# Mixed quarters of the feed-forward activations: t1 and t4 summed on TensorE like t2, ahead of the products of keys 3 and 4

## The chip, the core and the metric

The kernel runs on one core of a Trainium2 chip. The metric is device time of one execution in microseconds (us); lower is better. The engines are TensorE (PE, with PEld for its weight loads), VectorE (DVE), ScalarE (ACT), GpSimd (POOL) and SyncE (SP, which here only issues DMAs).

## What is computed

One decoder layer on a sequence of 1024 tokens with width 1024: attention and a state-space branch side by side, merged by gates and an output projection, and then a feed-forward block. The change lies in the feed-forward block. Of the reference it is these lines:

```
hn = rmsnorm(h, norm_ffn[i])
gate, up = jnp.split(hn @ w_ffn_in[i], 2, axis=-1)
h = h + (jax.nn.silu(gate) * up) @ w_ffn_out[i]
```

with `D_FF` = 2816, all in float32.

## The kernel before

Every product of the kernel is made of float32 operands that are split into a high part, rounded to the format fp32r, and a low part, the rest (`split`, L187: a cast on ACT, then a subtraction on DVE). `product` (L798) makes three matmuls for each block of 128 contracted rows: high with high, high with low, low with high.

The feed-forward products use a scheme of seven products instead of eight for a 2 x 2 block product. The normalized activations, transposed, lie in SBUF as quarters: `b11` and `b21` are the two halves of the features for tokens 0 to 511, `b22` is the second half of the features for tokens 512 to 1023, and `t3` is `b22` less the first half for those tokens; `norm_h` (L1106) makes these four, one block of 128 tokens at a time. From them come three mixed quarters: `t2 = b11 + t3`, `t1 = b22 - t2`, `t4 = b21 - t2`. Each is a tile of high and low parts, 128 partitions x 4 x 512 columns, in the dictionary `X`. The weights of a unit, 256 columns of `w_ffn_in`, are read in four quarters too (`raw_f`, later `raw_fg` for gate and `raw_fu` for up), and mixed on DVE into four sums (`sf`, `first_sums`). The seven products have the keys `11`, `12`, `2`, `3`, `1`, `22` and `4`; keys `11`, `12`, `3` and `4` need no mixed quarter of the activations but `t3`, key `2` needs `t2`, key `1` needs `t1`, key `22` needs `t4` (`FOR_B`, L796).

Units come in pairs, u = 0 for gate and u = 1 for up. The first pair (names ending in `_e`) is begun early, in the block that starts at L1098. Its keys `11` and `12` (banks `ch_e` and `si_e`, weights `we`) run between the last transposes of `norm_h`. Then stand, in the code's order: `t2`; for each u the loads, the sums, the operands (`wf`) and the products of keys `3` and `4` (banks `th_e` and `ex_e`); then operands and the quarters `t1` and `t4`. `first_units` (L1254) does the rest of the first pair: copies of the finished banks into cells (`c_e`, on ACT), then keys `2`, `1` (again in `ch_e`) and `22` (in `th_e`). From the second pair on `ffn_unit` (L1275) does a unit (names with `fg` and `fu`).

`mixed` (L833) makes a mixed quarter. For `t2` it sums on PE: for each of four groups of 512 columns it multiplies the high and low parts of both terms by an identity matrix, `one_r`, into one bank, four matmuls in all; ACT and DVE split the bank into the parts of `t2`, and ACT copies it once more, whole, into a page `t2f`. For `t1` and `t4` it works on DVE alone, on two halves of 1024 columns: high part of the other term less the page of `t2`, plus its low part, into a page (`t1f`, `t4f`), then a split.

The banks of PSUM, 128 partitions x 512 columns, are handed out in turn within four tags: `m` and `s` with two each, `x` with three and `q` with one. `th_e` of both units and `ex_e` of u = 0 are in `x`, `ex_e` of u = 1 is in `q`. Pages, the copies of the residual stream, the early weights and the raw weights of u = 1 share the pool `big` of eight tiles. A scheduler sets the order of the instructions on each engine from the code's order and the buffers; each engine then takes its own list strictly in that order.

Of the kernel before, what the change touches and what calls it, by code (L numbers as in the profile page):

```python
# [9 lines left out]
F32R = mybir.dt.float32r  # L10
I32 = mybir.dt.int32
BF16 = mybir.dt.bfloat16
AF = mybir.ActivationFunctionType
ALU = mybir.AluOpType
# [3 lines left out]
P = 128  # L18
# [28 lines left out]
def hybrid_layer_kernel(ctx: ExitStack, tc: tile.TileContext, x, meta_tokens, norm_mix, w_in, q_norm, k_norm,  # L47
                        attn_sinks, lam_re, lam_im, log_dt, ssm_b_re, ssm_b_im, ssm_c_re, ssm_c_im, ssm_d,
                        w_glu, attn_branch_norm, ssm_branch_norm, w_out, norm_ffn, w_ffn_in, w_ffn_out, out):
    nc = tc.nc  # L50
    x, out = x[0], out[0]
# [12 lines left out]
    def bank(name, tag=None):  # L64

        if tag is None:
            tag = "mmss"[turn[0] % 4]
            turn[0] += 1
        return ps.tile([P, 512], F32, tag=tag, bufs=BANKS[tag], name=name)
# [16 lines left out]
    ident = const.tile([P, P], F32, name="ident")  # L86
    make_identity(nc, ident)
    one_r = const.tile([P, P], F32R, name="one_r")
# [98 lines left out]
    def split(hi, lo, src):  # L187
        nc.scalar.copy(hi, src)  # L188
        nc.vector.tensor_tensor(out=lo, in0=src, in1=hi.bitcast(F32), op=ALU.subtract)
# [28 lines left out]
    with sbuf("p1", 2) as p1:  # L218
# [43 lines left out]
        pt = bank("lamT", "x")  # L262
# [26 lines left out]
        for b, (k, n) in enumerate([(ks[:, b, :], P) for b in range(8)] + [(ksm, NMETA)]):  # L289
            k = k.rearrange("p (h d) -> p h d", d=HD)  # L290
# [20 lines left out]
        t1, t2 = t12[:, 0:8], t12[:, 8:16]  # L311
# [91 lines left out]
    with sbuf("pp", 1) as pp:  # L403
# [26 lines left out]
        for what in range(2):  # L430
            raw = bc[what][:GRP].rearrange("g a b -> g (a b)")
            X, Y = ((XB, YB), (XC, YC))[what]
            for hh in range(2):
                pt = bank(f"bcT{what}{hh}", "x")
# [16 lines left out]
        for blk in range(8):  # L451
# [20 lines left out]
            for hh in range(2):  # L472
                pt = bank(f"bpT{blk}{hh}", "x")
# [14 lines left out]
            for e in range(2):  # L488
                for j in range(2):
                    o = bank(f"v{blk}{e}{j}", "q" if j else "x")  # L490
                    for k in range(2):
                        g = e + 4 * j + 2 * k
                        nc.tensor.matmul(o[:, k * NCH:(k + 1) * NCH], bpt[:, g * P:g * P + P], ut[:, g, :],
                                         start=True, stop=True)
# [277 lines left out]
    m = sp.tile([P, 2, 2, GRP // 2], F32, tag="cm", name="m")  # L772
# [33 lines left out]
    def tt_(out, in0, in1, op, eng=nc.vector):  # L806
        eng.tensor_tensor(out=out, in0=in0, in1=in1, op=op)  # L807

    X = {}
# [7 lines left out]
    def x_pair(key):  # L817

        t = rows_a(f"X{key}")
        X[key] = [t[:, 4 * p:4 * p + 4, :] for p in range(2)]  # L820
# [10 lines left out]

    full = {}

    def mixed(key, a, b, op, tag="s"):


        if key == "t2":
            for k in range(4):
                pt = bank(f"{key}_{k}", tag)
                for i, v in enumerate((X[b][0], X[b][1], X[a][0], X[a][1])):  # L840
                    nc.tensor.matmul(pt, one_r, v[:, k, :], start=(i == 0), stop=(i == 3))
                if k % 2 == 0:
                    full[k] = page(f"{key}f{k}").rearrange("p (k n) -> p k n", k=2)
                split(X[key][0][:, k, :], X[key][1][:, k, :], pt)
                nc.scalar.copy(full[k // 2 * 2][:, k % 2, :], pt)
            return
        for k in (0, 2):
            t = page(f"{key}f{k}").rearrange("p (k n) -> p k n", k=2)
            hi, lo = (X[a][p][:, k:k + 2, :].bitcast(F32) for p in range(2))
            tt_(t, hi, full[k], op)  # L850
            tt_(t, t, lo, ALU.add)
            split(X[key][0][:, k:k + 2, :], X[key][1][:, k:k + 2, :], t)
# [54 lines left out]
    for blk in (0, 4, 1, 5, 2, 6, 3, 7):  # L907
# [13 lines left out]
        for hh in range(2):  # L921
            o = bank(f"y{blk}{hh}")
            for k in range(4):
                g = 4 * hh + k
                nc.tensor.matmul(o[:, k * P:(k + 1) * P], ut[:, g, 2:], tp[:, :, g * 16:g * 16 + 16],
                                 start=True, stop=False)
                nc.tensor.matmul(o[:, k * P:(k + 1) * P], ss[:, g // 2, g % 2, :], ct[:, g, :],
                                 start=False, stop=True)
            nc.scalar.activation(
                out=z[:, :, 64 * hh:64 * hh + 64].rearrange("p t (g c) -> p g t c", c=16),  # L930
                in_=o.rearrange("p (g t c) -> p g t c", g=4, t=T), func=AF.Gelu_apprx_tanh)
# [13 lines left out]
    def page(name):  # L945
        return big.tile([P, D], F32, tag="s", name=name)

    with sbuf("mp", 2) as mp:
# [94 lines left out]
        for u in two:  # L1043
            for key in ("11", "12"):
                glu_step(*u, key, ops[u], True)
        mixed("t2", "t3", "b11", ALU.add)
        prepare(ua, "2", "3", "4")
        prepare(ub, "22", "2", "3", "4")
# [3 lines left out]
        for key, t, a in (("2", None, None), ("22", "t4", "b21"), ("1", "t1", "b22")):  # L1052
            if t:
                mixed(t, a, "t2", ALU.subtract)
            for u in two:
                if key == "1":
                    prepare(u, "1")
                glu_step(*u, key, ops[u], True)
# [41 lines left out]
    with sbuf("op", 2) as op_:  # L1100
        g_ffn = op_.tile([P, D], F32, tag="g", bufs=1, name="g_ffn")
        nc.scalar.dma_start(out=g_ffn, in_=norm_ffn[0:1, :].to_broadcast([P, D]))
        ssq = op_.tile([P, 8, 2], F32, tag="ssq", bufs=1, name="ssq")
        h2 = [None] * 8

        def norm_h(b):  # L1106
# [89 lines left out]
        def first_operands(u, keys, a, sums):  # L1196
            for key in keys:
                if key == "3":
                    src = op_.tile([P, 512], F32, tag="xs", bufs=3, name=f"sf3_{u}").rearrange("p (k n) -> p k n", k=4)
                    tt_(src, a["11"], a["21"], ALU.subtract)  # L1200
                elif key == "22":
                    src = a["22"]
                else:
                    src = sums[key]
                t = parts_of(pool_w.tile([P, 2, 512], F32R, tag="w", name=f"wf{u}{key}"))
                split(*t, src)
                first_ops[u][key] = t
# [9 lines left out]

        for key in ("t2", "t1", "t4"):
            x_pair(key)
        mixed("t2", "t3", "b11", ALU.add, "x")  # L1220
        for u in range(2):
            banks[u] |= {"3": bank(f"th_e{u}", "x"), "4": bank(f"ex_e{u}", "q" if u else "x")}
            banks[u]["22"] = banks[u]["3"]
# [6 lines left out]
                step_(u, first_ops[u], key, True, f"e{u}")  # L1230
            first_operands(u, ("2",), quarters[u], sums[u])
        first_operands(0, ("1",), quarters[0], sums[0])
        mixed("t1", "b22", "t2", ALU.subtract)
        first_operands(1, ("1",), quarters[1], sums[1])
        for u in range(2):
            first_operands(u, ("22",), quarters[u], sums[u])
        mixed("t4", "b21", "t2", ALU.subtract)
    big_cm.__exit__(None, None, None)

    with sbuf("fp", 2) as fp:  # L1240
# [213 lines left out]
```

## Time and profile before

| what | value |
|---|---|
| median of three runs | 1692.6 us (1685.52, 1692.6, 1692.88) |
| the profiled execution: its own time | 1688.96 us |
| its span, first to last instruction | 1687.2 us |
| mean granted TensorE clock | 0.974 |
| TensorE busy | 1577.3 us, 93% |
| VectorE busy | 1251.0 us, 74% |
| ScalarE busy | 738.6 us, 44% |
| GpSimd busy | 295.6 us, 18% |
| DMA | 196.93 MB, mean 117 GB/s |

The span leaves out what lies around the instructions, 1.8 us here. Busy time of PE is modelled and overlaps, since matmuls are pipelined; from one start to the next is what a matmul costs in a run of them. [...] The time of each stage is read from the rows below, counted from the span's start.

### The profile page before, as it was taken

The page shows a single profiled execution, that of the slowest core. Times are in us where ns is not written, and L with a number is a line of the kernel's source. Part 1 is how long each engine was busy: PE and PEld are TensorE (multiplying, and loading weights), DVE is VectorE, ACT ScalarE, POOL GpSimd, SP SyncE. Part 2 cuts the span into 40 slices and gives each one's busy share as a digit, 9 for nine tenths or more (in the row PEclk, how much of TensorE's full clock was granted, in tenths as well). Part 3 has the DMA queues.
Part 4 walks back from the last instruction along what each step waited for, and adds up shares of the span by engine and source line. Part 5 has one row for each costly group of instructions (what it writes and reads, how often), then busy time and mean ns, then how long its engine had stood idle before and what let it go on. Part 6 is the DMA issues. An engine that isn't in the chain of part 4 may idle for free.

```text
span 1687.2 us, 22176 instructions
## 1 busy us (share of the span) xinstructions
PE 1577.3 (93%) x7938; PEld 1304.0 (77%) x7938; DVE 1251.0 (74%) x2415; ACT 738.6 (44%) x1439; POOL 295.6 (18%) x237
## 2 busy tenths in 40 slices
PE   7999878989989999989997997999999999789999
PEld 5788768778867788877885785888888888568887
DVE  7769986999986698668767588865666664399773
ACT  5333425878885321565432334433333333333330
POOL 0001203343322000000000000111111121356441
PEclk9999989999999999999997998999999999999999
DMA  5264442011012873721243342423333331575432
GB/s 191 62 131 133 137 154 76 11 42 42 20 51 59 293 223 111 230 71 63 75 132 124 114 162 64 136 82 106 94 112 101 110 113 46 216 273 194 136 104 76
DMA packets 165950, 196.93 MB, mean 117 GB/s; under 512 B 12576, under 2 KB 117024, under 8 KB 165712
## 3 DMA queue, kind: packets, MB, share of 16 engines
q1 hardware_dynamic: 156240, 179.75, 33.0%
q10 hardware_dynamic: 8288, 11.01, 2.0%
q0 software_dynamic: 1312, 4.75, 0.8%
q8 instruction: 63, 1.03, 0.3%
q14 instruction: 47, 0.39, 0.1%
HBM read 140.62 MB, written 54.85 MB: 116 GB/s over the span
## 4 chain that ended last, share of the span: by engine, by line
PE 52%; DVE 18%; DMA 7%; issue 4%; ACT 3%; SPq 0%; ACTq 0%; DVEq 0%
PE ch_fg L803 6%; PE ch_fu L803 6%; PE wo L124 5%; PE ch L803 4%; PE ch_z L803 4%; PE th_fg L803 3%; PE th_fu L803 3%; PE si L803 3%; PE th_z L803 2%; PE q L124 2%; DVE pr L652 2%; PE si_fg L803 2%; PE si_fu L803 2%; PE g L124 1%; DVE A L807 1%
## 5 line engine op out<-in xcount | busy, mean ns | idle before, releaser
L124 PE MATMUL g<-xn,wh_g 128*128 128x512 f32 x512 | 166.3, 405 | 1.1 <-ACT sg L537 1.1
L803 PE MATMUL ch<-B,A 128*128 128x512 f32 x528 | 127.2, 397 | 15.2 <-ACT B L1386 9.1
L803 PEld LDWEIGHTS ch<-B,A 128*128 128x128 f32 x528 | 100.8, 192 | 39.1 <-ACT B L1386 8.2
L124 PEld LDWEIGHTS g<-xn,wh_g 128*128 128x128 f32 x512 | 97.6, 193 | 24.8 <-ACT sg L537 1.9
L124 PE MATMUL q<-wh_q,xn 128*128 128x256 f32 x512 | 103.6, 290 | 5.5 <-ACT qp L609 5.5
L124 PE MATMUL g<-xn,wl_g 128*128 128x512 f32 x256 | 102.7, 402 | 0.0
L803 PE MATMUL si<-B,A 128*128 128x512 f32 x396 | 92.5, 389 | 0.0
L124 PE MATMUL wo<-wh_o,mt 128*128 128x512 f32 x256 | 83.3, 405 | 9.4 <-ACT mt L188 7.5
L124 PE MATMUL u<-xn,wh_u 128*128 128x272 f32 (+2 forms) x384 | 91.7, 332 | 0.0
L124 PEld LDWEIGHTS q<-wh_q,xn 128*128 128x128 f32 x512 | 83.7, 193 | 7.1 <-ACT qp L609 5.9
L803 PEld LDWEIGHTS si<-B,A 128*128 128x128 f32 x396 | 74.3, 188 | 15.4
L1386 ACT CAST A<-rawa 128x1536 fp32r<-128x1536 f32 (+1 forms) x28 | 38.5, 1373 | 100.1 <-issue 49.5
L807 DVE TENSOR_TENSOR A<-rawa,A 128x1536 fp32r<-128x1536 f32 (+1 forms) x28 | 69.2, 2472 | 13.0 <-ACT A L1386 13.0
L124 PE MATMUL q<-wl_q,xn 128*128 128x256 f32 x256 | 73.7, 288 | 0.0
L658 ACT ACTIVATE pr<-pr,mn 128x272 f32<-128x272 f32 (+1 forms) x128 | 64.9, 508 | 16.1 <-DVE mn L652 13.3
L807 POOL TENSOR_TENSOR a<-c,c_fg 128x512 f32<-128x512 f32 x10 | 15.9, 1585 | 315.7 <-DVE c L807 211.1
L124 PEld LDWEIGHTS u<-xn,wh_u 128*128 128x128 f32 x384 | 66.0, 196 | 5.6
L807 POOL TENSOR_TENSOR B<-t,B 128x1536 fp32r<-128x1536 f32 (+1 forms) x16 | 59.2, 3711 | 58.5 <-ACT B L1386 58.5
L124 PEld LDWEIGHTS wo<-wh_o,mt 128*128 128x128 f32 x256 | 49.6, 195 | 20.4 <-ACT mt L188 10.1
L1065 POOL DMA_DIRECT2D pa<-pa_d x4 | 3.1, 778 | 353.3 <-PE ch_z L803 353.3
L124 PE MATMUL u<-xn,wl_u 128*128 128x272 f32 (+2 forms) x192 | 63.0, 330 | 0.0
L807 DVE TENSOR_TENSOR h2o<-h2o,ch 128x512 f32<-128x512 f32 x64 | 42.4, 680 | 27.3 <-PE ch L803 24.3
(459 smaller groups left out, 4217.6 us busy)
## 6 DMA issues: line engine op xcount, KB each, us to landing
rawa<-act_d SPq DMA_DIRECT2D x21, 768.0 KB
raw_fg<-in_w_ffn_in_dram SPq DMA_DIRECT2D x20, 512.0 KB
raw_fu<-in_w_ffn_in_dram SPq DMA_DIRECT2D x20, 512.0 KB
rawb<-in_w_ffn_out_dram SPq DMA_DIRECT2D x6, 1536.0 KB
act_d<-a SPq DMA_DIRECT2D x33, 256.0 KB
raw_g<-in_w_in_dram SPq DMA_DIRECT2D x16, 512.0 KB
raw_z<-in_w_glu_dram SPq DMA_DIRECT2D x16, 512.0 KB
act_d<-c_fg SPq DMA_DIRECT2D x30, 256.0 KB
```

The costliest lines, as they stand in the source:

```text
L124: nc.tensor.matmul(o, lhs(kb, a), rhs(kb, b), start=(kb == 0 and i == 0), stop=(kb == n - 1 and i == 2))
L652: nc.vector.tensor_tensor_reduce(out=pr[:, h, :n], in0=o[:, :n], in1=mask, scale=1.0, scalar=nsink[:, kv * 4 + h:kv * 4 + h + 1], op0=ALU. ...
L658: nc.scalar.activation(out=pr[:, h, :n], in_=pr[:, h, :n], func=AF.Exp, scale=-1.0, bias=mn[:, h:h + 1], accum_out=den[:, h:h + 1])
L803: nc.tensor.matmul(o, lhs(kb, a), rhs(kb, b), start=(first and kb == 0 and i == 0), stop=(kb == n - 1 and i == 2), skip_group_check=not first)
L807: eng.tensor_tensor(out=out, in0=in0, in1=in1, op=op)
L1065: nc.gpsimd.dma_start(out=pa[h][i], in_=pa_d[4 * i:4 * i + 4, :, 512 * h:512 * h + 512] .rearrange("f p n -> p f n"))
L1386: nc.scalar.copy(hi, src)
```

## The change

`t1` and `t4` are now made like `t2`, by a new function `summed`: for each group of 512 columns four matmuls into a bank of tag `x`, the terms' high and low parts with `one_r` for the term that is added and `minus`, a negated identity that ACT makes, for the one that is taken away. The pages `t2f`, `t1f` and `t4f` of the feed-forward block are gone. In the code all three quarters now stand ahead of the weight operands and the products of keys `3` and `4`. The function `mixed` is left for the other place that uses it, where its operations are the same as before.

```diff
+    def summed(key, terms, tag, keep=None):
+
+        for k in range(4):
+            pt = bank(f"{key}_{k}", tag)
+            parts = [(m, X[a][p][:, k, :]) for m, a in terms for p in range(2)]
+            for i, (m, v) in enumerate(parts):
+                nc.tensor.matmul(pt, m, v, start=(i == 0), stop=(i == len(parts) - 1))
+            split(X[key][0][:, k, :], X[key][1][:, k, :], pt)
+            if keep:
+                keep(k, pt)
...
+        minus = op_.tile([P, P], F32R, tag="minus", bufs=1, name="minus")
+        nc.scalar.activation(out=minus, in_=ident, func=AF.Copy, scale=-1.0)
...
         for key in ("t2", "t1", "t4"):
             x_pair(key)
-        mixed("t2", "t3", "b11", ALU.add, "x")
+        summed("t2", ((one_r, "b11"), (one_r, "t3")), "x")
+        summed("t1", ((one_r, "b22"), (minus, "t2")), "x")
+        summed("t4", ((one_r, "b21"), (minus, "t2")), "x")
...
         first_operands(0, ("1",), quarters[0], sums[0])
-        mixed("t1", "b22", "t2", ALU.subtract)
         first_operands(1, ("1",), quarters[1], sums[1])
         for u in range(2):
             first_operands(u, ("22",), quarters[u], sums[u])
-        mixed("t4", "b21", "t2", ALU.subtract)
```

On PE, from the last group of `t2` on, the order before is this (`Xb110` and `Xb111` are the high and low parts of `b11`, `Xb220` and `Xb221` those of `b22`, `Xt3` and `Xt2` hold both parts of `t3` and `t2`; the digit behind `th_e` and `ex_e` is the unit):

```order
L841 MATMUL t2_3_10054<-Xb110_9162,one_r_92 128x512
L841 MATMUL t2_3_10054<-Xb111_9163,one_r_92 128x512
L841 MATMUL t2_3_10054<-Xt3_9704,one_r_92 128x512 x2
L803 MATMUL th_e0_10062<-Xt3_9704,wf03_10077 128x512 x2
L803 MATMUL ex_e0_10063<-Xb220_9166,wf04_10080 128x512
L803 MATMUL ex_e0_10063<-Xb221_9167,wf04_10080 128x512
L803 MATMUL th_e0_10062<-Xt3_9704,wf03_10077 128x512 x10
```

And in the changed kernel, at the same place:

```order
L840 MATMUL t2_3_10051<-Xt3_9706,one_r_92 128x512 x2
L840 MATMUL t1_0_10058<-Xb220_9168,one_r_92 128x512
L840 MATMUL t1_0_10058<-Xb221_9169,one_r_92 128x512
L840 MATMUL t1_0_10058<-Xt2_10027,minus_9162 128x512 x2
L803 MATMUL ex_e1_10117<-Xb220_9168,wf14_10176 128x512
L803 MATMUL ex_e1_10117<-Xb221_9169,wf14_10176 128x512
L840 MATMUL t1_1_10065<-Xb220_9168,one_r_92 128x512
L840 MATMUL t1_1_10065<-Xb221_9169,one_r_92 128x512
L840 MATMUL t1_1_10065<-Xt2_10027,minus_9162 128x512 x2
```

The rest of `ex_e1` follows, then the other six groups of `t1` and `t4`, and only then `th_e0`, `ex_e0` and `th_e1`, whose banks are those that the last sums leave.

On DVE the order before, after `t2` has been split, is this (`wf03` is the operand of unit 0 for key 3, `wf04` for key 4, `wf02` for key 2; `sf` are the weight sums):

```order
L189 TENSOR_TENSOR wf03_10077<-sf3_0_10075,wf03_10077 128x512
L807 TENSOR_TENSOR sf1_10114<-raw_f10_10110,raw_f11_10112 128x512
L807 TENSOR_TENSOR t1f0_10157<-Xb220_9166,t2f0_10033 128x1024
L807 TENSOR_TENSOR t1f2_10162<-Xb220_9166,t2f2_10050 128x1024
L189 TENSOR_TENSOR wf04_10080<-sf4_0_10071,wf04_10080 128x512
L189 TENSOR_TENSOR wf02_10107<-sf0_10070,wf02_10107 128x512
L807 TENSOR_TENSOR sf1_10114<-sf1_10114,raw_f10_10110 128x512
L807 TENSOR_TENSOR t1f0_10157<-t1f0_10157,Xb221_9167 128x1024
L807 TENSOR_TENSOR t1f2_10162<-t1f2_10162,Xb221_9167 128x1024
```

In the changed kernel, from block 7 of the normalization on (`Xt3` and `Xb221` take its transposes):

```order
L807 TENSOR_TENSOR sf3_0_10127<-raw_f00_10118 128x512
L807 TENSOR_TENSOR sf4_1_10167<-raw_f11_10164,sf1_10166 128x512
L189 TENSOR_TENSOR Xt3_9706<-nt_h7_t3_9961,Xt3_9706 128x4x128
L189 TENSOR_TENSOR Xb221_9169<-nt_h7_b22_9968,Xb220_9168 128x4x128
L189 TENSOR_TENSOR wf03_10129<-sf3_0_10127,wf03_10129 128x512
L189 TENSOR_TENSOR wf04_10132<-sf4_0_10123,wf04_10132 128x512
L189 TENSOR_TENSOR wf02_10159<-sf0_10122,wf02_10159 128x512
L189 TENSOR_TENSOR Xt2_10027<-t2_0_10030,Xt2_10027 128x512
L807 TENSOR_TENSOR sf3_1_10171<-raw_f10_10162 128x512
L189 TENSOR_TENSOR Xt2_10027<-t2_1_10037,Xt2_10027 128x512
L189 TENSOR_TENSOR Xt2_10027<-t2_2_10044,Xt2_10027 128x512
```

Most of the weight sums have moved ahead of the last transposed block, three weight splits stand ahead of `t2`'s first group, and behind the third group stand five more, then the fourth group and those of `t1` and `t4`. On SP the load of the first half of unit 1's weights moved ahead of the store of the last block of the residual stream.

On ACT the order before, at the end of this part, is (`c11`, `c22`: cells of the copied banks; `w11_fg2`, `w12_fg2`: operands of the second pair):

```order
L188 CAST wf122_10173<-raw_f11_10112 128x512
L188 CAST w11_fg2_10313<-raw_fg20_10309 128x512
L188 CAST Xt4_10027<-t4f0_10176 128x1024
L188 CAST Xt4_10027<-t4f2_10181 128x1024
L188 CAST w12_fg2_10316<-raw_fg21_10311 128x512
L1259 COPY c11_e0_10191<-ch_e0_9973 128x512
L1261 COPY c22_e0_10192<-th_e0_10062 128x512
```

And in the changed kernel:

```order
L188 CAST Xt4_10029<-t4_3_10107 128x512
L188 CAST wf122_10215<-raw_f11_10164 128x512
L1269 COPY c11_e0_10223<-ch_e0_9975 128x512
L1271 COPY c22_e0_10224<-th_e0_10114 128x512
L1269 COPY c11_e1_10228<-ch_e1_10001 128x512
L188 CAST w11_fg2_10345<-raw_fg20_10341 128x512
```

The copies of the first pair's banks moved ahead of the casts of the second pair's weights; the cast of `w12_fg2` now comes later still.

## Rows read from the trace of the kernel before

**Rows 1.** The page, busy time, share of the span and instructions of TensorE and its loads.

```profile
PE 1577.3 (93%) x7938; PEld 1304.0 (77%) x7938; DVE 1251.0 (74%) x2415; ACT 738.6 (44%) x1439; POOL 295.6 (18%) x237
```

**Rows 2.** Stages: stretch, length; busy (instructions) by engine; PEclk granted, DMA share, GB/s.

```profile
1021.11:1026.10 4.99, 4.53 (x19) 2.75 (x17) 3.39 (x6) 3.56 (x7) 0.00 (x0) 1.00 0.00 0
...
1030.08:1052.31 22.23, 16.76 (x49) 12.26 (x49) 22.23 (x27) 10.67 (x17) 0.00 (x0) 0.74 0.23 71
1052.31:1068.77 16.46, 16.46 (x73) 13.62 (x74) 13.76 (x23) 10.91 (x19) 0.00 (x0) 1.00 0.35 111
1068.77:1150.00 81.23, 81.23 (x359) 67.01 (x358) 54.48 (x73) 28.92 (x51) 13.20 (x8) 1.00 0.33 106
1028.20:1034.90 6.70, 4.82 (x11) 3.80 (x12) 6.02 (x9) 1.66 (x3) 0.00 (x0) 0.50 0.26 78
...
1041.90:1048.60 6.70, 5.64 (x13) 4.46 (x14) 6.70 (x10) 1.74 (x4) 0.00 (x0) 0.50 0.04 7
```

**Rows 3.** PE's timeline: start, length, instruction, [idle before, releaser].

```profile
1021.11 0.72 PE L841 MATMUL t<-Xb,one_r 128*128 128x512 f32 x2
...
1022.32 0.50 PE L841 MATMUL t<-Xt,one_r 128*128 128x512 f32 x1 [0.23 <-DVE Xt L189]
1022.65 0.63 PE L841 MATMUL t<-Xb,one_r 128*128 128x512 f32 x2
...
1023.59 0.63 PE L841 MATMUL t<-Xb,one_r 128*128 128x512 f32 x2
...
1024.91 0.73 PE L841 MATMUL t<-Xb,one_r 128*128 128x512 f32 x2 [0.23 <-ACT t2f L845]
...
1030.08 1.22 PE L803 MATMUL th_e<-Xt,wf 128*128 128x512 f32 x2 [3.98 <-ACT wf L188]
...
1039.61 0.73 PE L803 MATMUL th_e<-Xt,wf 128*128 128x512 f32 x2 [1.49 <-ACT wf L188]
...
1042.96 4.63 PE L803 MATMUL th_e<-Xt,wf 128*128 128x512 f32 x10 [2.10 <-DVE wf L189]
1047.40 3.04 PE L803 MATMUL ex_e<-Xb,wf 128*128 128x512 f32 x10
1052.31 3.02 PE L803 MATMUL ch_e<-Xt,wf 128*128 128x512 f32 x12 [1.88 <-ACT c_e L1259]
...
1065.14 2.88 PE L803 MATMUL ch_e<-Xt,wf 128*128 128x512 f32 x12
1067.86 1.07 PE L803 MATMUL th_e<-Xt,wf 128*128 128x512 f32 x4
1068.77 0.39 PE L803 MATMUL si_fg<-Xb,w_fg 128*128 128x512 f32 x1
```

**Rows 4.** The chain that ended last, in order of time: start, length, what.

```profile
1035.43 2.27 DVE t1f L807 x2
...
1047.08 3.97 DMA raw_fg<-in_w_ffn_in_dram
...
1051.77 0.49 ACT c_e L1259
```

**Rows 5.** DVE's timeline: block 7 of the normalization (two rows), t1, weight splits.

```profile
1017.75 0.75 DVE L1126 SCALAR_TENSOR_TENSOR xs<-h,ri,g_ffn 128x512 f32<-128x512 f32 x1 [3.10 <-PE nt_h_t L1133]
...
1021.57 0.69 DVE L189 TENSOR_TENSOR Xt<-nt_h_t,Xt 128x512 fp32r<-128x512 f32 x1 [1.27 <-ACT Xt L188]
...
1031.27 2.35 DVE L807 TENSOR_TENSOR t1f<-Xb,t2f 128x1024 f32<-128x1024 f32 x2
...
1043.97 2.49 DVE L189 TENSOR_TENSOR wf<-sf,wf 128x512 fp32r<-128x512 f32 x4
```

**Rows 6.** ACT's timeline: casts of weight sums.

```profile
1029.41 1.66 ACT L188 CAST wf<-sf 128x512 fp32r<-128x512 f32 x3 [1.34 <-DVE sf L807]
```

**Rows 7.** SP's timeline, the loads of unit 1's raw weights; and a stage (columns as rows 2).

```profile
1011.43 3.00 SPq L1188 DMA_DIRECT2D raw_f<-in_w_ffn_in_dram  x2
...
1017.00:1018.00 1.00, 1.00 (x11) 0.91 (x10) 0.25 (x1) 0.25 (x1) 0.00 (x0) 1.00 0.03 8
```

More of the change, by code (lines that the diff above doesn't have):

```diff
@@ L832, in hybrid_layer_kernel, with mixed, keep @@
     full = {}
-    def mixed(key, a, b, op, tag="s"):
+    def summed(key, terms, tag, keep=None):
[7 more added lines that the diff above has]
+                keep(k, pt)
+    def mixed(key, a, b, op):
         if key == "t2":
[L838 to L841, printed above, removed]
+            def keep(k, pt):
                 if k % 2 == 0:
                     full[k] = page(f"{key}f{k}").rearrange("p (k n) -> p k n", k=2)
-                split(X[key][0][:, k, :], X[key][1][:, k, :], pt)
                 nc.scalar.copy(full[k // 2 * 2][:, k % 2, :], pt)
+            summed(key, ((one_r, b), (one_r, a)), "s", keep)
             return
```

## The prediction

> **What bounds the kernel now.** TensorE (PE) is busy for 93% of the span [rows 1], so I looked first for the stretch near the change where it is not. The stage table shows it: from 1021.11 us, where the sum t2 begins, to 1068.77, where the products of the next pair of feed-forward units begin, the clock falls to 0.50 in two stretches, and from 1030.08 to 1052.31 PE is busy for 16.8 of 22.2 us, while from 1052.31 on it is full at clock 1.00 [rows 2]. [...] Next I read PE's own timeline [rows 3]. It names the waits: 0.23 and 0.23 within t2, then 3.98, 1.49, 2.10 and 1.88, together 9.91 us. All four long ones end with a weight operand (wf) or with a copy of a bank (c_e), not with PE. Last I read the chain of waits [rows 4]. It leaves PE at t2's end and runs through VectorE's (DVE's) mixed quarters, through the second half of the weights of the next units (raw_fg, 3.97 us) and through ScalarE (ACT), until a copy lets PE go on at 1052.31. So this stretch is set by DVE and by what stands in order behind it. That DVE is the late one is seen from its rows, where two operations of t1 on 1024 columns, 2.27 us in the chain, 1.14 each, stand ahead of weight splits for which PE is waiting [rows 4, 5].
>
> **What the stretch is worth.** It holds 16 sum matmuls, 48 products of keys 3 and 4 (th_e, ex_e) and 72 more products. At the full clock a product starts 2.72/12 = 0.227 us after the one before, and a sum 0.94/4 = 0.235 [rows 3]. So the work is 16 x 0.235 + 120 x 0.227 = 31.0 of 47.66 us. Waits take 9.9. The remaining 6.8 is the half clock, where ten products of th_e took 4.44 us [rows 3], which is 0.444 each.
>
> **The change, part by part.** *Added on PE:* 32 sum matmuls of 512 columns (four banks, four matmuls, for t1 and t4). The nearest row is the same instruction in t2, 0.235 us [rows 3], so 7.5 us. All of it lies on PE's path, because PE will have no idle time to put it in once the waits are gone. The work becomes 38.5 us.
> [...]
>
> *Removed from DVE:* eight additions or subtractions on 1024 columns, 8 x 1.14 = 9.1 us [rows 4]. The four low-part splits on 1024 columns become eight on 512, 4 x 1.14 against 8 x 0.60, no difference. *Removed from ACT:* four copies of t2 into pages; four casts become eight smaller ones; about 2 us less. ACT is busy for 10.7 of 22.2 us here [rows 2], so I cost that at nothing.
>
> *Moved:* without pages for t2, t1 and t4, the sums of the weight quarters (sf) stand earlier on DVE, two of them around the normalization of block 5, two in block 7 and three around its end. The order of DVE now shows weight splits ahead of t2's evacuation; in the order before, t1 stood between those splits. In block 7 DVE has 3.10 us of idle time [rows 5] and needs 1.2 for the two sums. They wait for a load that SP now issues at about 1011.4 instead of 1014.0. Such a load takes at most 3.5 us: the one issued at 1014.0 had ended by 1017 to 1018, where the DMA share is 0.03 [rows 7]. So it lands at 1015 and DVE is free again by 1016.3, ahead of 1017.75, where it is next needed. I cost this at nothing; if the load landed as late as before, it would be 0.8 us, and the difference that now stands ahead of block 7's last subtraction could cost its own 0.60. The minus-identity is one small ACT operation long before.
>
> *Added waits on PE.* t2's banks now empty behind weight work. DVE has two differences ahead of the last transposed block; they cost 1.2 us, of which the 1.27 of idle time [rows 5] hides more than half: 0.5 late. The first bank of t2 then waits for three splits of 0.60 on DVE, and the three casts of 1.66 on ACT beside them [rows 5, 6]: t2's fourth group, which takes the first one's bank, starts about 0.9 later. The first group of t1 waits about 0.3 for the second bank. With the 0.46 that was there, 2.2 us. After that a group of four takes PE 0.94, ACT about 0.5 and DVE 0.60, so evacuation keeps up, and products of ex_e stand between the groups for the rest. The lower bound of the waits is 0.46 (none added), the upper 4.44 (the long wait of 3.98 stays) with one more stretch of 6.7 us at 0.50, which costs 3.35.
>
> *The sum:* 38.5 + 2.2 = 40.7 us instead of 47.66: 7.0 us gained. By the lower bound 8.7, by the upper 1.4. Behind the stretch PE is full from 1068.77 on [rows 2], so it is paced by itself, and starting it 7 us earlier moves the end as much. What is late next would be the weights of the next units, but DVE has 9 us less to do ahead of them, and raw_fg's second load no longer waits for splits that stood behind t1. ACT's copies of the banks now stand ahead of the cast that waited for that load.
>
> The profiled execution took 1688.96 us, so it would take 1682.0. The median of the three runs, 1692.6, is 3.6 above the profiled one; against it the forecast is **1685.6 us**. What a measurement of this kernel can tell from no change is about 0.5%, 8.5 us; the gain is just below that.
>
> **The rivals.** *A. The forecast:* PE runs through from t1 on, at 1.00. It gives 5 to 9 us.
>
> *B. One wait stays.* If t2's evacuation is slower behind the five weight splits than I take it, PE waits about 4 us once more, and the clock falls as it did at 1028 [rows 2]. The gain is then 1.4 us, or 3.6 if only the clock falls: 1689 to 1691. Against it: ACT and DVE come to t2 without t1's and t4's load.
>
> *C. Slower: the clock falls under short waits.* From t2 on PE works in groups of four that turn through three banks, with waits of 0.3 to 1 us between them. If that lets the clock fall, it is PE's own time, since nothing else is late now. Every matmul then takes 0.227 us more, so 31 of them eat the gain, and from there it is slower. If it held for the 48 sums, the 12 products between them and a further 6.7 us as at 1028 (15 matmuls at half clock), 75 matmuls lose 17.0 us: 10.0 slower, 1702.6. For it: two such stretches occur in this place now [rows 2]. Against it: they followed waits of 3.98 us and of 1.49 and 2.10 close together, while the t2 groups with two waits of 0.23 ran at 1.00, as the row from 1021.11 to 1026.10 shows [rows 2, 3].
> [...]
>
> *D. It doesn't shorten the stretch.* In the chain the last link is a load and a copy behind it [rows 4], not t4. If PE still waited for that copy until 1052, the products after it would start no earlier: 1692.6. Against it: the order on ACT puts the copies ahead of that cast.
>
> **How the numbers follow.** A has 0.77. Its center lies 1.5 us short of the bound, and the runs of before alone differ by 7.4 us, so I split it into 0.37 faster and 0.40 same. B has 0.12 and D 0.06, both same. C has 0.05, slower. Together 0.37 faster, 0.58 same, 0.05 slower. The range reaches from the lowest run less the greatest gain, 1685.5 - 8.7 = 1677, to the highest less the smallest, 1692.9 - 1.4 = 1691.5; it takes in A and B and leaves out most of C and D.
>
> **What would show it.** In the profile of the changed kernel: no wait of PE over 1.5 us between t2 and the next pair's first product; clock 1.00 throughout; about 40.7 us from t2's first matmul to that product; eight groups of sums at about 0.94 us each; DVE without operations on 1024 columns in this stretch; and a time behind the stretch that is the same as before. A half clock within the stretch shows B or C, by whether a wait of 4 us comes before it; a wait for a copy of a bank at the first ch_e product shows D. If the stretch is 7 us shorter and the end isn't, then something behind it, the loads of the output projection above all, was the bound. A gain over 9 us would mean that the runs lose more to the clock here than the profiled one does.

## The result, and the profile after

The changed kernel takes 1676.47 us (median of 4 runs, 1670.14 to 1678.87), the kernel before 1692.03 in the same comparison (1685.52 to 1692.88). The ratio is 0.9908, with an interval of 0.9888 to 0.9928: 15.6 us less. The forecast was 1685.6 with a range from 1677 on, so the gain is twice the 7.0 us that were expected and the time lies just below the range.

The profiled execution took 1678.87 us (span 1677.1, mean granted clock 0.977 of full speed). Its busy line, beside [rows 1], has the 32 additional matmuls:

```profile
PE 1580.1 (94%) x7970; PEld 1309.0 (78%) x7970; DVE 1239.1 (74%) x2411; ACT 737.5 (44%) x1440; POOL 298.3 (18%) x237
```

PE's timeline of the changed kernel, in the columns of [rows 3], where the change was made:

```profile
1023.66 0.71 PE L840 MATMUL t<-Xb,one_r 128*128 128x512 f32 x2
...
1025.45 0.50 PE L840 MATMUL t<-Xt,one_r 128*128 128x512 f32 x1 [0.81 <-DVE Xt L189]
...
1028.45 0.73 PE L840 MATMUL t<-Xb,one_r 128*128 128x512 f32 x2 [0.64 <-DVE Xt L189]
...
1034.39 0.62 PE L840 MATMUL t<-Xb,one_r 128*128 128x512 f32 x2
...
1039.96 2.92 PE L803 MATMUL th_e<-Xt,wf 128*128 128x512 f32 x12
...
1048.16 5.60 PE L803 MATMUL ch_e<-Xt,wf 128*128 128x512 f32 x24
...
1064.48 1.75 PE L803 MATMUL ch_fg<-Xb,w_fg 128*128 128x512 f32 x7
```

Two waits are left, 0.81 and 0.64 us; the four long ones of [rows 3] are gone. Six groups of sums run from 1034.39 to 1039.96 without a pause, 24 matmuls at 0.232 us. The stretch is 1064.48 - 1023.66 = 40.82 us.

So far this is the forecast. To find the rest, I cut both executions at the same instructions: the first product of the second pair of units (`ch_fg` or `si_fg`), the first product of the output projection (`ch`), the last one. Stages of the changed kernel, in the columns of [rows 2]: t2, the rest of the stretch, the feed-forward pairs, the output projection:

```profile
1023.66:1029.65 5.99, 4.54 (x19) 2.75 (x17) 5.99 (x11) 4.76 (x10) 0.00 (x0) 1.00 0.27 88
1029.65:1064.48 34.83, 34.83 (x153) 28.64 (x153) 26.05 (x41) 21.61 (x39) 0.00 (x0) 1.00 0.27 86
...
1064.48:1456.63 392.15, 382.23 (x1681) 314.65 (x1679) 233.15 (x310) 132.98 (x232) 69.63 (x44) 1.00 0.30 100
...
1456.63:1672.70 216.07, 212.91 (x924) 173.97 (x924) 162.44 (x154) 72.23 (x54) 105.18 (x28) 0.99 0.50 177
```

The same two last stages of the kernel before:

```profile
1068.77:1461.25 392.48, 382.53 (x1681) 314.55 (x1679) 234.36 (x311) 133.27 (x233) 69.66 (x44) 1.00 0.31 101
...
1461.25:1682.70 221.45, 214.05 (x923) 175.10 (x924) 165.28 (x154) 72.00 (x54) 105.34 (x28) 0.98 0.48 173
```

The pairs are equal within 0.3 us. The output projection, 400 us behind the change and untouched by it, is 5.4 us shorter: the same instructions on TensorE, VectorE (DVE) and GpSimd in the same order, less waiting, and DVE busy for 2.8 us less over the same 154 entries. With the stretch's 6.8 and the 0.3 of the pairs that makes 12.5 us. (The stages ahead of the change took 2.55 us longer in this execution, as the starts 1021.11 and 1023.66 show; in repeats they go either way.) Where the 5.4 us lie is seen in PE's waits in the output projection; before:

```profile
1461.25 2.08 PE L803 MATMUL ch<-B,A 128*128 128x512 f32 x4 [7.79 <-ACT B L1386]
...
1475.85 0.47 PE L803 MATMUL ch<-B,A 128*128 128x512 f32 x1 [1.27 <-ACT B L1386]
1476.52 2.79 PE L803 MATMUL ch<-B,A 128*128 128x512 f32 x11 [0.20 <-DVE h2o L807]
1480.95 1.66 PE L803 MATMUL ch<-B,A 128*128 128x512 f32 x6 [1.64 <-DVE h2o L807]
...
1509.51 9.99 PE L803 MATMUL ch<-B,A 128*128 128x512 f32 x36 [3.79 <-DVE h2o L807]
```

and after:

```profile
1456.63 2.07 PE L803 MATMUL ch<-B,A 128*128 128x512 f32 x4 [7.76 <-ACT B L1396]
...
1470.52 0.47 PE L803 MATMUL ch<-B,A 128*128 128x512 f32 x1 [0.42 <-DVE h2o L807]
1471.20 4.45 PE L803 MATMUL ch<-B,A 128*128 128x512 f32 x17 [0.21 <-DVE h2o L807]
...
1500.34 8.42 PE L803 MATMUL ch<-B,A 128*128 128x512 f32 x36 [1.39 <-DVE h2o L807]
...
1558.73 8.46 PE L803 MATMUL ch<-B,A 128*128 128x512 f32 x36 [0.78 <-DVE h2o L807]
```

Behind the first product the waits are, besides one of 0.37 us in both, 6.90 us before (1.27, 0.20, 1.64, 3.79) and 2.80 after (0.42, 0.21, 1.39, 0.78). And the 36 products behind the wait of 3.79 us took 9.99 instead of 8.42, since part of them ran at the lower clock: it was 0.50 from 1509.5 to 1512.8 us, and 0.83 on average from 1509.5 to 1519.5. 4.1 + 1.6 = 5.7, about the 5.4 that the stage lost. PE waits for banks that DVE empties into `h2o`, so the question is why DVE is late there before and not after.

### The profile page after: what moved, and what is told of

Its sections match the earlier page's. It is cut to its first block, busy times and chain, and to the rows that moved or that the text cites. A ratio compares the mean times of both kernels' runs of the same rounds, so it can differ in the third digit from the quotient of the medians.

```text
span 1677.1 us, 22235 instructions
## 1 busy us (share of the span) xinstructions
PE 1580.1 (94%) x7970; PEld 1309.0 (78%) x7970; DVE 1239.1 (74%) x2411; ACT 737.5 (44%) x1440; POOL 298.3 (18%) x237
## 4 chain that ended last, share of the span: by engine, by line
PE 54%; DVE 16%; DMA 7%; ACT 3%; issue 3%; POOL 0%; SPq 0%; ACTq 0%; DVEq 0%
PE ch_fg L803 6%; PE ch_fu L803 6%; PE ch L803 6%; PE wo L124 5%; PE si L803 4%; PE ch_z L803 4%; PE th_fg L803 3%; PE th_fu L803 3%; PE th_z L803 2%; DVE pr L652 2%; PE q L124 2%; PE si_fu L803 2%; PE si_fg L803 2%; PE g L124 1%; DVE pr L664 1%
## 5 line engine op out<-in xcount | busy, mean ns | idle before, releaser
L1396 ACT CAST A<-rawa 128x1536 fp32r<-128x1536 f32 (+1 forms) x28 | 38.5, 1374 | 96.3 <-issue 44.3
L124 PEld LDWEIGHTS wo<-wh_o,mt 128*128 128x128 f32 x256 | 49.8, 196 | 20.4 <-ACT mt L188 10.1
```

Of the source, the lines that this page charges most:

```text
L124: nc.tensor.matmul(o, lhs(kb, a), rhs(kb, b), start=(kb == 0 and i == 0), stop=(kb == n - 1 and i == 2))
```

## The experiments

Each kernel ran on one chip beside the kernel before, which had medians of 1690.09, 1690.26 and 1689.49 us in the three groups (e1 to e4, e5 to e8, e9 to e12). "Stretch" is from t2's first sum to the second pair, "stage" the output projection from its first product to its last, both from the profiled execution.

**Is it in every execution, and in which part?** e1 and e2 are the two kernels again, unaltered.

> The kernel before, a second time, to see what two profiled executions of one kernel differ by. All theories: ratio 1.00. Theory P (the change shortens only the stretch from t2 to the second pair's first product, by 6.8 us, and the rest of the measured 15.6 us is scatter of other stages) expects here a stretch of 47 to 48 us again, but an output projection stage (from its first product to the last) that can come out anywhere from 215 to 222 us. Theory Q (the change also shortens the output projection stage, 221.5 us before and 216.0 after) expects that stage at 220 to 223 us again.

> The changed kernel, a second time. Theory P: 6 to 9 us below before (ratio about 0.995 to 0.996), stretch 40.8 us, output projection stage anywhere from 215 to 222 us. Theory Q: 12 to 16 us below before (ratio 0.991 to 0.993), stretch 40.8, output projection stage again 215 to 217 us.

Measured: e1 1688.83 us, ratio 1.0001 (0.9985 to 1.0017), stretch 47.5, stage 221.6. e2 1677.03, ratio 0.9919 (0.9899 to 0.9940), stretch 40.8, stage 216.1. Both differences come back to within 0.2 us. The gain is not scatter: theory P falls, and Q stands as a description without a cause.

**The place alone.** e3 leaves t1 and t4 on DVE and moves them ahead:

```diff
         mixed("t2", "t3", "b11", ALU.add, "x")
+        mixed("t1", "b22", "t2", ALU.subtract)
+        mixed("t4", "b21", "t2", ALU.subtract)
...
-        mixed("t1", "b22", "t2", ALU.subtract)
...
-        mixed("t4", "b21", "t2", ALU.subtract)
```

> Of the change only the place: t1 and t4 still on DVE, but written ahead of the weight operands and the products of keys 3 and 4. If TensorE is what shortened the stretch, this shortens nothing: DVE has as much to do and the first operand that PE waits for comes later, stretch 48 to 53 us, time 0 to 5 us above before. If the place alone did it, stretch 41 to 44 us and 4 to 7 us below before.

Measured: 1693.51 us, ratio 1.0014 (0.9998 to 1.0030), stretch 51.9, stage 221.6. PE waits once, 16.75 us, for a weight operand behind both quarters on DVE. Standing early isn't what gains; the sums must leave DVE.

**Half of the change.** e4 sums t1 alone on PE; t4 stays on DVE in its old place.

```diff
         mixed("t2", "t3", "b11", ALU.add, "x")
+        summed("t1", ((one_r, "b22"), (minus, "t2")), "x")
...
-        mixed("t1", "b22", "t2", ALU.subtract)
```

> Half of the change: t1 on TensorE and early, t4 on DVE at its old place, with t2's pages kept. If DVE's work on PE's path is what counts, about half of the stretch's gain or more: 42 to 45 us, 3 to 5 us below before by theory P. Theory Q, where the later stage gains from an earlier start, expects 6 to 10 us below before.

Measured: 1682.84 us, ratio 0.9960 (0.9944 to 0.9976), stretch 43.2, stage 222.2. Two thirds of the stretch's gain come with t1, and nothing of the stage's. So the stage doesn't follow from an earlier start (e4 reached it at about the same time as the changed kernel, 1454.43 us), nor from t1's sums by themselves.

**What differs behind the change.** With the instructions the same, I compared the transfers. Over the whole program the trace has a queue of kind "instruction", q8, with 63 packets of 16 KB. I took it for TensorE's own program: 7938 matmuls in 63 packets are 126 for each, and e6 below, with 128 matmuls more than the kernel before, has 64 packets. I call such a packet a piece. One takes about 1 us of one of the 16 DMA engines: the 2.1% of 16 engines over 3 us in the row below are 1.0. The transfers of 3 us, from 7 us behind the first `ch` product on, while the loads of `h2o` run (the DMA share is 1.05 there in both kernels); before:

```profile
q1 hardware_dynamic: 625, 1.19, 103.4%
q8 instruction: 1, 0.02, 2.1%
```

and after:

```profile
q1 hardware_dynamic: 638, 1.22, 104.9%
```

Before, a piece starts 8.2 us behind that product. After, 32 matmuls more lie ahead of it, a quarter of a piece, and the piece falls 11.4 us ahead of the product, where the DMA share is 0.25 (1444 to 1447 us). (That is 19.6 us sooner and not the 7 that 32 matmuls take; 7.79 of the difference are PE's wait ahead of the product, which lies in between.) In e4, with 16 more, it falls at 6.0. What the piece delays first is seen at SyncE, which issues the sixteen loads of `h2o` one behind the other. Its second issue, before and after:

```profile
1469.59 1.22 SPq L1356 DMA_DIRECT2D h2o<-h_d  x1
```

```profile
1464.97 0.37 SPq L1366 DMA_DIRECT2D h2o<-h_d  x1
```

Before, it starts 8.34 us behind the product, with the piece, and takes 0.85 us longer; in e1 and e2 the same issue takes 1.10 and 0.37. e5 to e8 test this by shifting the pieces and nothing else: short matmuls ahead of `th_e`, into a bank that the next product starts anew. No other instruction moves on any engine. e5 is the kernel before with 32 of them, e6 to e8 the changed kernel with 96, 32 and 64.

```diff
             banks[u]["22"] = banks[u]["3"]
+        for _ in range(32):
+            nc.tensor.matmul(banks[0]["3"][:, 0:16], one_r, one_r[:, 0:16], start=True, stop=True)
```

> The kernel before, with 32 short matmuls (128 x 16 columns, identity times identity, overwritten by the next product) at the place where TensorE waits 3.98 us ahead of th_e; nothing else moves on any engine. Theory F, fetch: TensorE's program comes in pieces of 16 KB through one of the 16 DMA engines, a piece for every 128 matmuls, about 1 us each; in the kernel before one piece falls 8.2 us behind the first product of the output projection, among the loads of h2o, and in the changed kernel, whose 32 more matmuls shift the pieces, it falls 11.3 us ahead of that product. By F this kernel has the piece about 11 us ahead too, the stretch stays at 47.6 us (the short matmuls lie in the wait), the stage of the output projection falls from 221.6 to about 216, and the time to about 1684.5 (ratio 0.997). Theory G: the stage is shorter for another reason that the sums bring (buffers, what precedes it); then the stage stays at 221.6 and the ratio is 1.000.

> The changed kernel with 96 short matmuls in the same place, ahead of th_e, so that the 32 + 96 extra ones make one whole piece of the program and the pieces fall again as in the kernel before. TensorE has no wait there now, so the stretch grows by what they take, an estimated 6 us. Theory F: the piece falls about 8 us behind the first product of the output projection, the stage is 221.6 us, and the time about 1677 + 6 + 5.5 = 1688.5. Theory G: the stage stays at 216 and the time is about 1683.

> The changed kernel with 32 short matmuls there: the pieces move another quarter, to about 18 us ahead of the first product of the output projection and 20 to 24 behind it. The stretch grows by about 2 us. Theory F: no piece among the loads of h2o, so the stage is 216, unless a piece at 20 to 24 us hits the later loads; time about 1679. Theory G: 216 in any case.

> The changed kernel with 64 short matmuls there: the pieces fall about 26 us ahead of the first product of the output projection and about 15 behind it, when the loads of h2o have all been issued. The stretch grows by about 4 us. Theory F: the first add into h2o waits as in the changed kernel, the stage is 216 to 218, and the time about 1681. Theory G: 216.

| kernel | time, us | ratio | stretch | stage | pieces nearest, us from the first product |
|---|---|---|---|---|---|
| e5, before + 32 | 1683.03 | 0.9955 (0.9938 to 0.9973) | 47.5 | 216.1 | -11.2, 31.4 |
| e6, change + 96 | 1703.57 | 1.0072 (1.0059 to 1.0084) | 59.6 | 222.6 | 7.9, 40.2 |
| e7, change + 32 | 1688.51 | 0.9985 (0.9969 to 1.0000) | 44.4 | 222.0 | -20.8, 24.8, 54.9, 84.7 |
| e8, change + 64 | 1687.96 | 0.9986 (0.9975 to 0.9998) | 52.8 | 216.5 | -27.7, 18.6, 46.1 |

e5 gets the stage's gain without any part of the change, and e6 takes it from the changed kernel. Theory F is shown, in both directions; G falls. The long stages are those with a piece at 6.0 to 8.2 us (before, e1, e3, e4, e6), the short ones those without (after, e2, e5, e8).

e7 has no piece there, and its stage is long all the same; there another piece falls among later loads. It starts at 84.7 us, 5.7 us after SyncE issued a load of `rawb` (in the changed kernel the DMA share is 1.00 from 84.4 to 88.2 us). DVE then waits 2.35 us for that load, in the changed kernel, whose piece falls at 88.2, 1.13. DVE's rows of e7:

```profile
1547.44 1.76 DVE L807 TENSOR_TENSOR t<-rawb,t 128x1536 f32<-128x1536 f32 x1 [2.35 <-DMA rawb<-in_w_ffn_out_dram]
...
1555.30 4.87 DVE L807 TENSOR_TENSOR A<-rawa,A 128x1536 fp32r<-128x1536 f32 x1
```

and the same two of the changed kernel:

```profile
1543.48 1.76 DVE L807 TENSOR_TENSOR t<-rawb,t 128x1536 f32<-128x1536 f32 x1 [1.13 <-DMA rawb<-in_w_ffn_out_dram]
...
1551.34 1.74 DVE L807 TENSOR_TENSOR A<-rawa,A 128x1536 fp32r<-128x1536 f32 x1
```

Behind the late load the operation on `rawa` takes 4.87 instead of 1.74 us, and PE waits 3.50 us in the third of the four parts of the projection. That a piece can hit later loads stood in the expectation only as an "unless", and for a piece at 20 to 24 us. The stretches of e6 and e8 grew by 18.8 and 12.0 us where I had expected 6 and 4, figures that no run had shown; the last section has what the short matmuls took.

**How 1 us becomes 5.5.** DVE's rows in the output projection, of e6 (the piece among the loads):

```profile
1490.37 2.90 DVE L807 TENSOR_TENSOR A<-rawa,A 128x1024 fp32r<-128x1024 f32 x1
...
1507.72 1.75 DVE L807 TENSOR_TENSOR A<-rawa,A 128x1536 fp32r<-128x1536 f32 x1
1509.39 5.05 DVE L807 TENSOR_TENSOR t<-rawb 128x1536 f32<-128x1536 f32 x1
...
1516.16 4.80 DVE L807 TENSOR_TENSOR A<-rawa,A 128x1536 fp32r<-128x1536 f32 x1
```

and the same four of e5 (no piece there):

```profile
1478.88 1.60 DVE L807 TENSOR_TENSOR A<-rawa,A 128x1024 fp32r<-128x1024 f32 x1
...
1495.37 5.05 DVE L807 TENSOR_TENSOR A<-rawa,A 128x1536 fp32r<-128x1536 f32 x1
1500.34 1.75 DVE L807 TENSOR_TENSOR t<-rawb 128x1536 f32<-128x1536 f32 x1
...
1503.80 1.74 DVE L807 TENSOR_TENSOR A<-rawa,A 128x1536 fp32r<-128x1536 f32 x1
```

The same operation takes 1.75 or 5.05 us, and what differs beside it is what GpSimd (POOL) does. In the kernel before, where the pattern is e6's, DVE and POOL have these rows:

```profile
1475.02 1.45 DVE L807 TENSOR_TENSOR h2o<-h2o,ch 128x512 f32<-128x512 f32 x2 [2.92 <-DMA h2o<-h_d]
1476.38 0.68 DVE L807 TENSOR_TENSOR h2o<-h2o,si 128x512 f32<-128x512 f32 x1
1476.98 3.31 DVE L807 TENSOR_TENSOR A<-rawa,A 128x1024 fp32r<-128x1024 f32 x1
...
1494.75 1.75 DVE L807 TENSOR_TENSOR A<-rawa,A 128x1536 fp32r<-128x1536 f32 x1
1496.42 5.05 DVE L807 TENSOR_TENSOR t<-rawb 128x1536 f32<-128x1536 f32 x1
...
1503.18 4.40 DVE L807 TENSOR_TENSOR A<-rawa,A 128x1536 fp32r<-128x1536 f32 x1
```

```profile
1472.13 7.08 POOL L807 TENSOR_TENSOR B<-t,B 128x1024 fp32r<-128x1024 f32 x3 [4.64 <-ACT B L1386]
...
1494.92 4.93 POOL L807 TENSOR_TENSOR B<-rawb,B 128x1536 fp32r<-128x1536 f32 x1 [1.41 <-ACT B L1386]
...
1502.45 3.51 POOL L807 TENSOR_TENSOR B<-rawb,B 128x1536 fp32r<-128x1536 f32 x1 [2.60 <-ACT B L1386]
```

and the changed kernel these:

```profile
1469.69 1.46 DVE L807 TENSOR_TENSOR h2o<-h2o,ch 128x512 f32<-128x512 f32 x2 [2.21 <-DMA h2o<-h_d]
...
1471.66 1.68 DVE L807 TENSOR_TENSOR A<-rawa,A 128x1024 fp32r<-128x1024 f32 x1
```

```profile
1467.52 8.10 POOL L807 TENSOR_TENSOR B<-t,B 128x1024 fp32r<-128x1024 f32 x3 [4.64 <-ACT B L1396]
```

DVE starts its first `h2o` add 13.77 us behind the first product before and 13.06 after: 0.7 us for the piece. POOL makes three operations at that time in both kernels. Before, DVE's next operation starts close behind the start of the third, takes 3.31 us and ends 1.1 us behind POOL's row. After, it starts within the second, takes 1.68, and it is POOL that is held up: 8.10 us for its three instead of 7.08. Later the order in which the two engines meet is different too, and DVE's three operations on 1536 columns take 1.75 + 5.05 + 4.40 = 11.2 us instead of the 8.5 of e5's pattern. Together that makes 0.7 + 1.6 + 2.7 = 5.0 us by which DVE is later when PE needs its banks. The pattern comes back: the three take 11.2 to 11.7 us in before, e1, e3, e4 and e6, and 8.5 to 8.6 in after, e2, e5, e7 and e8.

In the two long ones DVE seems to wait for POOL: it ends at 1501.47 and 1507.58, both times 1.62 us behind the end of POOL's operation (1499.85 and 1505.96), and where POOL is idle a DVE operation on 1536 columns takes 1.74 (the one at 1511.09). The 4.87 of e7 ends 1.62 us behind one as well (1560.17 and 1558.55), and so does the 5.05 at 1488.23 in the changed kernel (1493.28 and 1491.66). Where DVE's operation started first, at 1494.75, it was POOL's that took longer, 4.93 us for the 3.51 of the one at 1502.45. The `h2o` adds, which have one input in PSUM, keep their 0.68 while POOL runs (the one at 1476.38). That these meetings turn 0.7 us into 5 is read from the rows; no run takes them away and leaves the rest as it was.

e9 to e12 try to take the effect away: in e9 (kernel before) and e10 (changed) the low parts of B in the first of the four parts are made on DVE, so that POOL is idle there; in e11 and e12 ScalarE issues the first four loads of `h2o`, so that they land earlier.

```diff
-                B[key] = operand(b, nc.gpsimd, f"B{key}_{j0}")
+                B[key] = operand(b, nc.gpsimd if j0 else nc.vector, f"B{key}_{j0}")
```

```diff
-                nc.sync.dma_start(out=h2[b][:, cols], in_=h2_d[b][:, cols])
+                (nc.scalar if q == "11" else nc.sync).dma_start(out=h2[b][:, cols], in_=h2_d[b][:, cols])
```

> The kernel before, whose low parts of the weights B in the first of the four pieces of the output projection (seven differences on 1024 columns) are made on VectorE instead of GpSimd. Theory H, on how a fetch of 1 us becomes 5.5 us: the late h2o holds VectorE up by 1 us, and its next operations then run beside GpSimd's, which makes them last up to three times as long (3.29 us where one alone takes 1.22), so VectorE is 4 us late when TensorE needs the banks that it empties. By H, with GpSimd idle there, the late h2o costs about 1 us, and this kernel and its twin on the changed kernel differ by at most 2 us in the stage of the output projection. VectorE gets 8.5 us more work in the first 25 us, so the stage itself may be anywhere between 214 and 224. Rival K: the fetch costs its 5.5 us in another way (TensorE's own instructions are late, or the lower clock behind a wait); then the two differ by 4 us or more here too.

> The changed kernel with the same edit, the pieces of TensorE's program falling 11 us ahead of the first product of the output projection. By H its stage is at most 2 us shorter than that of its twin on the kernel before, by K 4 us or more. If VectorE carries the additional work in its idle time, the stage is 214 to 216 and the time 1675 to 1677; if it doesn't, up to 1685.

> The kernel before, whose first four loads of h2o are issued by ScalarE instead of SyncE, so that they don't stand behind two loads that wait for VectorE. The order of some products and adds in the first piece of the output projection moves with it. By F and H what counts is that h2o lands ahead of VectorE's first add; the loads should land by about 8 us behind the first product instead of 13.6, so that a fetch at 8.2 us no longer holds VectorE up: stage 214 to 217, time about 1685. If the stage stays at 221 to 222, the fetch hits another load, or it is not the wait for h2o that costs.

> The changed kernel with the same edit. The first add into h2o waited 2.04 us here, so VectorE is ahead by up to that much: stage 213 to 216, time 1674 to 1677. By F and H it differs from its twin on the kernel before by the stretch alone, 6.8 us.

| kernel | time, us | ratio | stretch | stage |
|---|---|---|---|---|
| e9, before, low parts on DVE | 1693.37 | 1.0023 (1.0011 to 1.0034) | 49.1 | 223.8 |
| e10, changed, low parts on DVE | 1686.08 | 0.9982 (0.9969 to 0.9995) | 40.8 | 225.6 |
| e11, before, h2o by ScalarE | 1693.01 | 1.0018 (1.0005 to 1.0031) | 47.5 | 224.9 |
| e12, changed, h2o by ScalarE | 1685.22 | 0.9978 (0.9965 to 0.9991) | 40.8 | 224.8 |

Within each pair the stage now differs by 1.8 and 0.1 us, though the kernels before still have their piece at 7.3 and 7.7 us and the changed ones at -11.2, and in the first pair it is the kernel before that is shorter. K's forecast of 4 us or more fails, H's of at most 2 us doesn't, and the change is worth 7.3 and 7.8 us here, about its stretch alone. But it is no clean test: all four stages are longer than 216, where I had expected most of them shorter, and PE has other long waits in them (4.37 us in e9, 3.50 in e10, 3.05 in e11, 4.66 in e12), behind which a delay of 1 us could vanish. And part of K holds in the kernel before: 1.6 of its 5.4 us are the lower clock behind the wait of 3.79. In e12 DVE's first add starts 10.8 us behind the first product, two earlier than in the changed kernel, and the stage is still 224.8: the edit moved the order of products and adds too, and DVE's operations meet POOL's more often, as these rows of e12 show.

```profile
1472.23 2.54 DVE L807 TENSOR_TENSOR A<-rawa,A 128x1024 fp32r<-128x1024 f32 x1 [1.88 <-ACT A L1396]
...
1475.89 2.20 DVE L807 TENSOR_TENSOR A<-rawa,A 128x1024 fp32r<-128x1024 f32 x1
...
1485.48 3.40 DVE L807 TENSOR_TENSOR A<-rawa,A 128x1024 fp32r<-128x1024 f32 x1
```

So landing early is not a gain by itself. What stays open is a rule for which meetings of DVE and POOL follow from which arrival time; the runs show only that the piece's place decides between 216 and 222 us with the program's order as it is. None of the kernels tried beats the changed one.

## Why the prediction was wrong

*The stretch: right.* Work 38.5 and waits 2.2 were forecast, 40.7; measured are 40.82, of it 1.45 of waits. So the work took 39.4, 0.9 more than forecast, all of it ahead of 1034.39, and the waits 0.7 less; that the sum came out to 0.1 us is in part luck. A sum matmul takes 0.232 us in the groups (0.235 taken), the clock is 1.00 throughout, where [rows 2] had two stretches at 0.50, the copies of the banks no longer hold up the first `ch_e` product, and DVE has no operation on 1024 columns there. The one t2 wait is larger than I took it from block 7's work, 0.81 for 0.5 + 0.23, and the wait for the first group's bank smaller, 0.64 for 0.9; the other two, 0.3 and 0.23, did not come.

*The rivals.* B (a wait of 4 us stays), C (the clock falls under short waits) and D (the copy still sets the end) are refuted by the same rows: waits of 0.81 and 0.64 us, clock 1.00. For C that means that here two waits between groups that turn through three banks did not lower the clock. That TensorE must be the engine was assumed, not weighed; e3 shows it (51.9 us with both quarters early on DVE).

*The step that failed:* "Behind the stretch PE is full from 1068.77 on [rows 2], so it is paced by itself, and starting it 7 us earlier moves the end as much", and with it "a time behind the stretch that is the same as before". The row for this ended at 1150 us [rows 2]. To 1461, where the output projection begins, the time stayed the same, 392.15 against 392.48. The output projection is not paced by PE alone: it held 6.9 us of waits and 3.3 us at clock 0.50. I had named "the loads of the output projection above all" as a possible bound, but only as something that could eat the gain, and took the 32 matmuls for 7.5 us on PE and nothing else. They had a second effect, through the transfer of the program: with 32 matmuls more, a piece of about 1 us of one DMA engine moved from 8.2 us behind the first product of the output projection to 11.4 us ahead of it, from a costly place to a harmless one. The stage gave 5.5 us (e5 alone has it), the stretch 6.8; that is 12.3 of the 13.1 to 15.6 us between the medians in the two comparisons, and within their intervals; what is left is not traced to a stage.

*The last clue was wrong too.* "A gain over 9 us would mean that the runs lose more to the clock here than the profiled one does": the clock is 1.00 in the stretch in every profiled execution of the changed kernel, and the surplus lies 400 us later.

The chance of 0.58 for no measurable difference came from a center just short of the bound; both parts together make 0.92%.

## What to carry to other kernels

When a gain is larger or smaller than its stage explains, cut both traces at the same instructions and compare every stage, also those that the change doesn't touch. Here 32 matmuls more moved the pieces of the program to other transfers, and the stage went from 221.5 to 216.1 us by that alone (e5); look in the list of transfers for the instruction queue in any stretch where the DMA share is near 1, and before crediting a change with a gain of a few us, shift the fetches alone with some short instructions in an idle place. Where VectorE and GpSimd work beside each other and TensorE waits for them, look at what their operations take there: here one of 1.74 us took up to 5.05, a delay of 0.7 us came out as 5.0, and between e11 and e12 the piece's place made 0.1.

## What the runs showed of the hardware that I had not expected

*Fetching the program cost other transfers time.* A 16 KB packet on q8 took about 1 us of one DMA engine, 63 of them per execution, and its place made 5.5 to 6.5 us of stage time: 216.1 with it elsewhere, 221.6, 222.6 and 222.0 with it among loads that were waited for. TensorE itself was not seen to wait for a packet: from the second pair of units on, PE's waits in the changed kernel end with ACT (9.9 us), DVE (2.8) or GpSimd (0.4). What was late beside one were loads: the second issue of `h2o` took 1.22 us with it and 0.37 without, and DVE's first add waited 2.92 us for its load before and 2.21 after.

*The clock fell while short matmuls ran.* In e6 96 matmuls of 16 columns ran without a pause, behind sums at clock 1.00, and took 16 us. The granted clock was 1.00 up to 1043.5, while the first of them ran, and 0.50 from 1043.6 to 1060.5; the first products behind them were slow too, 5.47 us for twelve where the changed kernel has 2.92. Without the short matmuls, in the changed kernel, the clock stays at 1.00 here (1043.5 to 1060.5). PE's row, and a stretch with its granted clock, 0.57 on average:

```profile
1038.62 16.02 PE L1237 MATMUL th_e<-one_r 128*128 128x16 f32 x96
```

```profile
1041.00:1060.00 19.00, 19.00 (x89) 17.84 (x89) 0.00 (x0) 0.01 (x1) 0.00 (x0) 0.57 0.00 1
```

PE counts as busy for the whole of those 19 us. With 32 of them (e7) the stretch grew by 3.6 us, at clock 1.00 throughout, which is 0.11 us each; with 64 (e8) it grew by 12.0, 10.1 of which ran at 0.50. I had taken 2 and 4, which no run had shown.
